# Two-block transformer on one core: the dense feed-forward products take the stream's high and low parts side by side

## The chip, the cores and the metric

One core of a Trainium2 chip runs the whole program in one launch. The metric is the device time of that core in microseconds; lower is better. The kernel before takes 2152.02 us, the median of three runs (2150.91 to 2152.64).

## What is computed

A sequence of 256 tokens of width 1024 goes through three layers. The first is a block with HGRN2 and block attention and a dense SwiGLU feed-forward of width 2816. The second layer has a mixer of four branches (pooling, short convolution, spatial gating, differential attention) and another dense feed-forward of 2816; the third has the same kind of mixer and a mixture of eight experts. Cut to what the change touches:

```
def swiglu(x, w_gate_up, w_down):
    g, u = jnp.split(x @ w_gate_up, 2, axis=-1)
    return (jax.nn.silu(g) * u) @ w_down
...
merged = (gates[:, :, 0] * (y_a @ w_branch_pool[layer])
          + gates[:, :, 1] * (y_b @ w_branch_conv[layer])
          + gates[:, :, 2] * (y_c @ w_branch_sgu[layer])
          + gates[:, :, 3] * (y_d @ w_branch_attn[layer]))
return merged @ w_out[layer]
```

All inputs are float32, and float32 precision is kept by splitting both operands of every large product into a rounded high part and a low remainder. A product is then three matmuls: weight-high with stream-high, weight-high with stream-low, weight-low with stream-high.

## The kernel before

**Weights.** Each weight element is used once. `load` brings 1 MB at a time into a raw buffer on SP's queue. `look_ahead` (line 417 is its subtraction, line 185 the helper that issues every ScalarE instruction) cuts a load into *pieces* of 1024 columns per partition: ScalarE copies a piece to `hi`, VectorE subtracts to get `lo`. Three pieces are kept ahead of TensorE, and `hi` and `lo` have four buffers each.

**Units.** The order of the work is written out by hand, with no scheduler: `unit` issues one piece's products, then the next piece's split, then whatever evacuations are pending (`flush`). A function put up with `defer` goes out one flush later. Each engine works its own list in that order and waits on semaphores for the others. Side work (attention heads, small mixers) is issued between units by generators.

**Dense feed-forward** (`ffn`, `residual`). The normalized stream `N.x` is held transposed, features on partitions, as four page pairs of high (`nh`) and low (`nl`), each 2 x 256 tokens. `chunk_t` makes 256 output columns: two pieces m = 0, 1 of 128 columns, for each of 8 contraction blocks k the three 256-column matmuls of `mm3t` (lines 502 to 504), with the weights as the stationary operand:

```
mm(out, hi[:, k, :], xh, start=r + k == 0, stop=False)
mm(out, hi[:, k, :], xl, start=False, stop=False)
mm(out, lo[:, k, :], xh, start=False, stop=r + k == kb - 1)
```

The two pieces lie in the two halves of one PSUM bank. There are 11 gate chunks and 11 up chunks in each of the two dense feed-forwards. The gate chunk is multiplied by the norm's factors (line 540) and goes through Silu; the up chunk is multiplied by them and by the gate (985), then split into `ah` and `al` (215). The first gate chunk, `chunk_late`, puts off its last two blocks, since the stream's last quarter comes late. `residual` then makes the down product over 22 blocks in four such chunks and adds each to the stream `self.x` (963), after which `norm_feed` prepares that quarter for the next norm. When `residual` ends an attention or mixer part instead (8 blocks), it begins with `chunk_late_pair` and feeds `ffn`.

**PSUM.** Eight banks: a pool of four that `gp` hands out (large products) and one of four that `sp` hands out (small products of heads, transposes, norms).

**Mixer's end** (`mixer`, `branch`, `gate_half`, line 565 to 567). The gates of the third and fourth branch's second half are still being made (`gate_half` holds two `gp` banks open over two units) while the four branch products run: `branch(0, 0)` and `branch(1, 0)` come between the two halves of gate 2. A branch takes two `gp` banks, 12 matmuls of 512 columns (24 for the fourth), and is evacuated one unit later by `gated` (line 916), which multiplies the gate with it:

```
gate_half(2, 0)
self.drain()
sigmoids(2)
branch(0, 0)
sigmoids(1)
branch(1, 0)
gate_half(2, 4, 1)
```

## Time and profile before

| | us |
|---|---|
| median of three runs | 2152.02 (2150.91 to 2152.64) |
| the profiled execution | 2152.17 |
| its span in the trace | 2150.4 |
| TensorE (PE) busy | 2134.0 (99%) |
| VectorE (DVE) busy | 1736.9 (81%) |
| ScalarE (ACT) busy | 1436.6 (67%) |
| granted TensorE clock, mean | 0.997 |

The span is what the trace covers; the profiled execution's own time has 1.8 us more around it. A row of the page's busy groups gives a line, engine, operation, output and inputs, the count, the busy time and the mean of one. Matmuls overlap, so a matmul's length in the trace is not its price: the distance from one start to the next is. In a matmul's row the moving operand stands first, then the stationary one.

### The profile page before, as it was taken

What the parts mean: (1) busy time and instruction counts of PE and PEld (TensorE: products, weight loads), DVE (VectorE), ACT (ScalarE), POOL (GpSimd) and SP (SyncE); (2) the same over time, 40 slices, a digit from 0 to 9 for tenths busy, and PEclk for the clock granted to TensorE, in tenths of its full rate; (3) what the DMA queues carried; (4) which work ended last, traced back from release to release, by engine and by line L of the source; (5) the groups of instructions that cost most, each with busy time, mean ns of one, the idle gap of its engine ahead of it and who ended that gap; (6) DMA issues with size and microseconds to landing.
All of it is one profiled execution on the core that took longest, in us unless ns stands there. A gap on an engine that the chain in (4) does not pass through costs nothing.

```text
span 2150.4 us, 32906 instructions
## 1 busy us (share of the span) xinstructions
PE 2134.0 (99%) x12243; PEld 1870.0 (87%) x12243; DVE 1736.9 (81%) x2424; ACT 1436.6 (67%) x2022; POOL 67.9 (3%) x90
## 2 busy tenths in 40 slices
PE   9999999999999999999999999999999999999998
PEld 9988889999987999999879788888888888888886
DVE  7877667655686766567867999999999999999997
ACT  6347645444556554445665888888887888888886
POOL 0000000003000000020000000000000000000200
PEclk9999999999999999999999999999999999999999
DMA  9444455546644555475475899999999999999995
GB/s 346 144 137 158 137 187 186 184 161 219 205 153 157 195 181 183 149 244 176 147 245 196 298 329 385 353 375 374 383 377 351 383 367 387 350 384 373 385 387 185
DMA packets 338280, 565.31 MB, mean 263 GB/s; under 512 B 14090, under 2 KB 117530, under 8 KB 338112
## 3 DMA queue, kind: packets, MB, share of 16 engines
q1 hardware_dynamic: 333616, 551.50, 73.7%
q0 software_dynamic: 4064, 11.05, 1.5%
q8 instruction: 98, 1.61, 0.3%
q10 hardware_dynamic: 432, 0.57, 0.1%
q14 instruction: 70, 0.57, 0.1%
HBM read 558.32 MB, written 4.75 MB: 262 GB/s over the span
## 4 chain that ended last, share of the span: by engine, by line
PE 97%; ACT 1%; DMA 1%; DVE 0%; issue 0%; SPq 0%; DVEq 0%; ACTq 0%
PE g L1755 9%; PE g L1757 9%; PE g L1756 9%; PE g L502 8%; PE g L503 8%; PE g L504 8%; PE g L565 7%; PE g L566 7%; PE g L567 7%; PE y L1778 5%; PE y L1779 5%; PE y L1780 5%; PE lev L1069 1%; PE at L1735 1%; PE xe L1674 1%; PE g L554 1%
## 5 line engine op out<-in xcount | busy, mean ns | idle before, releaser
L185 ACT ACTIVATE hi<-raw 128x1024 fp32r<-128x1024 f32 (+2 forms) x1223 | 1123.6, 934 | 586.1 <-PE g L503 196.8
L417 DVE TENSOR_TENSOR lo<-raw,hi 128x1024 fp32r<-128x1024 f32 (+2 forms) x1216 | 1273.5, 1074 | 237.5 <-ACT hi L185 202.4
L1755 PE MATMUL g<-hi,xe 128*128 128x512 f32 x896 | 353.8, 395 | 0.0
L1757 PE MATMUL g<-lo,xe 128*128 128x512 f32 x896 | 349.3, 390 | 0.0
L1756 PE MATMUL g<-hi,xe 128*128 128x512 f32 x896 | 349.0, 389 | 0.0
L502 PE MATMUL g<-nh,hi 128*128 128x256 f32 x1024 | 291.7, 285 | 0.0
L504 PE MATMUL g<-nh,lo 128*128 128x256 f32 x1024 | 289.8, 283 | 0.0
L503 PE MATMUL g<-nl,hi 128*128 128x256 f32 x1024 | 289.7, 283 | 0.0
L565 PE MATMUL g<-hi,nh 128*128 128x512 f32 x544 | 219.6, 404 | 0.2 <-DVE gt L916 0.2
L567 PE MATMUL g<-lo,nh 128*128 128x512 f32 x544 | 212.4, 390 | 0.0
L566 PE MATMUL g<-hi,nl 128*128 128x512 f32 x544 | 212.0, 390 | 0.0
L1757 PEld LDWEIGHTS g<-lo,xe 128*128 128x128 f32 x896 | 168.2, 188 | 35.9
L1756 PEld LDWEIGHTS g<-hi,xe 128*128 128x128 f32 x896 | 168.4, 188 | 33.4
L1755 PEld LDWEIGHTS g<-hi,xe 128*128 128x128 f32 x896 | 168.3, 188 | 33.4
L503 PEld LDWEIGHTS g<-nl,hi 128*128 128x128 f32 x1024 | 196.5, 192 | 0.2
L502 PEld LDWEIGHTS g<-nh,hi 128*128 128x128 f32 x1024 | 196.4, 192 | 0.2
L504 PEld LDWEIGHTS g<-nh,lo 128*128 128x128 f32 x1024 | 196.4, 192 | 0.0
L1778 PE MATMUL y<-hi,ah 128*128 128x512 f32 x448 | 175.8, 392 | 0.0
L1779 PE MATMUL y<-hi,al 128*128 128x512 f32 x448 | 174.5, 390 | 0.0
L1780 PE MATMUL y<-lo,ah 128*128 128x512 f32 x448 | 174.4, 389 | 0.0
L565 PEld LDWEIGHTS g<-hi,nh 128*128 128x128 f32 x544 | 102.4, 188 | 23.5 <-issue 3.2
L567 PEld LDWEIGHTS g<-lo,nh 128*128 128x128 f32 x544 | 102.1, 188 | 22.1
(421 smaller groups left out, 2797.2 us busy)
## 6 DMA issues: line engine op xcount, KB each, us to landing
raw<-in_moe_w_gate_up_dram SPq DMA_DIRECT2D x168, 1024.0 KB, 7.1
raw<-in_w_in_dram SPq DMA_DIRECT2D x90, 1024.0 KB, 5.1
raw<-in_moe_w_down_dram SPq DMA_DIRECT2D x88, 1024.0 KB, 5.9
raw<-in_moe_w_gate_up_dram SPq DMA_DIRECT2D x224, 256.0 KB, 7.2
raw<-in_moe_w_down_dram SPq DMA_DIRECT2D x96, 256.0 KB, 6.7
raw<-in_ffn_w_gate_up_dram SPq DMA_DIRECT2D x22, 1024.0 KB, 5.1
raw<-in_w_ffn_gate_dram SPq DMA_DIRECT2D x11, 1024.0 KB, 5.3
raw<-in_w_ffn_up_dram SPq DMA_DIRECT2D x11, 1024.0 KB, 5.4
```

The lines of the kernel that those rows point to most:

```text
L185: return self.nc.scalar.activation(out, in_, func, **kw)
L417: self.nc.vector.tensor_sub(l, x, h)
L502: mm(out, hi[:, k, :], xh, start=r + k == 0, stop=False)
L503: mm(out, hi[:, k, :], xl, start=False, stop=False)
L504: mm(out, lo[:, k, :], xh, start=False, stop=r + k == kb - 1)
L565: mm(ps[t], xh[:, s], hi[:, k, :], start=r + k == 0, stop=False)
L566: mm(ps[t], xl[:, s], hi[:, k, :], start=False, stop=False)
L567: mm(ps[t], xh[:, s], lo[:, k, :], start=False, stop=r + k == kb - 1)
L1755: mm(ps, xh, hi[:, k, :], start=first, stop=False)
L1756: mm(ps, xl, hi[:, k, :], start=False, stop=False)
L1757: mm(ps, xh, lo[:, k, :], start=False, stop=last)
L1778: mm(py, xh, hi[:, i, :], start=k == 0, stop=False)
```

## The change

The high and low part of the stream lie in one page, side by side (`gain` with `pairs`, `split_pair`), so that one 512-column matmul, `mm_hi`, makes weight-high with both parts; `mm_lo` then adds weight-low with stream-high, 256 columns, to the half that holds weight-high with stream-low. `chunk_pair` issues eight of the first and then eight of the second for a piece. Each piece has a bank of its own now, so a chunk holds two; `bank` takes one from each pool in turn. The two halves of a bank have to be added: in gate and up ScalarE copies one half out and VectorE adds the other (`halves`), in the down product (first three of four chunks) VectorE adds both halves to the stream. The fourth down chunk keeps `chunk_t`. Silu is put off by one more flush. In the mixers, `branch` takes its banks from the small products' pool.

```diff
--- before.py
+++ after.py
@@ -214,6 +214,18 @@
         self.copy(hi, x)
         self.defer(lambda: self.nc.vector.tensor_sub(lo, x, hi))
         return hi, lo
+
+    def split_pair(self, x):
+
+        pages = [self.pgv(2, T, dt=F32R, nm="a") for _ in range(2)]
+        for j, p in enumerate(pages):
+            self.copy(p[:, 0, :], x[:, j, :])
+
+        def rest():
+            for j, p in enumerate(pages):
+                self.nc.vector.tensor_sub(p[:, 1, :], x[:, j, :], p[:, 0, :])
+        self.defer(rest)
+        return pages
 
     def warm(self, n, x):
 
@@ -492,6 +504,9 @@
 
 
     def xb(self, x, k):
+        if isinstance(x[k // 2], list):
+            p = x[k // 2][k % 2]
+            return p[:, 0, :], p[:, 1, :]
         h, l = x[k // 2]
         return h[:, k % 2, :], l[:, k % 2, :]
 
@@ -512,22 +527,52 @@
                 self.unit(lambda hi, lo: self.mm3t(pv[:, m, :], hi, lo, x, r, min(8, kb - r), kb),
                           (lambda: evac(pv)) if last else None, width)
 
-    def chunk_late(self, x, evac, width=1):
-
-        ps = [self.gp()[:, :T] for _ in range(2)]
+    def mm_hi(self, out, hi, x, r, n):
+
+        for k in range(n):
+            p = x[(r + k) // 2][(r + k) % 2]
+            self.nc.tensor.matmul(out, hi[:, k, :], p.rearrange("p a t -> p (a t)"), start=r + k == 0, stop=False)
+
+    def mm_lo(self, out, lo, x, r, n, kb):
+
+        for k in range(n):
+            p = x[(r + k) // 2][(r + k) % 2]
+            self.nc.tensor.matmul(out[:, T:], lo[:, k, :], p[:, 0, :], start=False, stop=r + k == kb - 1)
+
+    def bank(self):
+        self.turns += 1
+        return self.sp() if self.turns // 2 % 2 else self.gp()
+
+    def chunk_pair(self, x, evac, kb=8):
+
+        ps = [self.bank() for _ in range(2)]
+
+        def products(hi, lo, m, r):
+            n = min(8, kb - r)
+            self.mm_hi(ps[m], hi, x, r, n)
+            self.mm_lo(ps[m], lo, x, r, n, kb)
+        for m in range(2):
+            for r in range(0, kb, 8):
+                last = m == 1 and r + 8 >= kb
+                self.unit(lambda hi, lo: products(hi, lo, m, r), (lambda: evac(ps)) if last else None)
+
+    def chunk_late(self, x, evac):
+
+        ps = [self.bank() for _ in range(2)]
         late = []
         for m in range(2):
-            run = self.stage(width)
-            hi, lo = self.ahead.pop(0)
-            self.mm3t(ps[m], hi, lo, x, 0, 6, 8)
-            late.append((hi, lo))
+            run = self.stage(1)
+            late.append(self.ahead.pop(0))
+            self.mm_hi(ps[m], late[m][0], x, 0, 6)
+            self.mm_lo(ps[m], late[m][1], x, 0, 6, 8)
             if m == 0:
                 self.look_ahead()
             self.flush()
             self.finish(run)
-        for k in range(6, 8):
-            for m, (hi, lo) in enumerate(late):
-                self.mm3t(ps[m], hi[:, k:, :], lo[:, k:, :], x, k, 1, 8)
+        for m, (hi, lo) in enumerate(late):
+            self.mm_hi(ps[m], hi[:, 6:, :], x, 6, 2)
+        for m, (hi, lo) in enumerate(late):
+            self.mm_lo(ps[m], lo[:, 6:, :], x, 6, 2, 8)
         self.look_ahead()
         self.pending.append(lambda: evac(ps))
 
@@ -609,8 +654,9 @@
                           (lambda i=i: evacs[i](ps[i])) if r else None, width)
 
 
-    def norm_begin(self, g):
+    def norm_begin(self, g, pairs=False):
         N = Norm()
+        N.pairs = pairs
         N.g, N.x = g, [None] * 4
         page = self.pg(nm="rs")
         N.rs, N.tmp = page[:, :T], page[:, T:]
@@ -629,12 +675,17 @@
     def gain(self, N, c):
 
         x = self.x[c]
-        hi, lo = N.x[c] = tuple(self.pgv(2, T, dt=F32R, nm="n" + s) for s in "hl")
+        if N.pairs:
+            N.x[c] = [self.pgv(2, T, dt=F32R, nm="n") for _ in range(2)]
+            hi, lo = ([p[:, i, :] for p in N.x[c]] for i in range(2))
+        else:
+            N.x[c] = tuple(self.pgv(2, T, dt=F32R, nm="n" + s) for s in "hl")
+            hi, lo = ([t[:, j, :] for j in range(2)] for t in N.x[c])
         gs = [N.g[:, 2 * c + j:2 * c + j + 1] for j in range(2)]
         for j in range(2):
-            self.copy(hi[:, j, :], x[:, j, :], scale=gs[j])
+            self.copy(hi[j], x[:, j, :], scale=gs[j])
         for j in range(2):
-            self.nc.vector.scalar_tensor_tensor(lo[:, j, :], x[:, j, :], gs[j], hi[:, j, :], op0=OP.mult, op1=OP.subtract)
+            self.nc.vector.scalar_tensor_tensor(lo[j], x[:, j, :], gs[j], hi[j], op0=OP.mult, op1=OP.subtract)
 
     def squares(self, N, c, e):
 
@@ -953,10 +1004,14 @@
 
     def residual(self, x, kb, g, between=None):
 
-        N = self.norm_begin(g)
+        N = self.norm_begin(g, kb == 8)
 
         def evac(c, ps):
-            if isinstance(ps, list):
+            if kb == KF and c < 3:
+                for h in (slice(T, 2 * T), slice(0, T)):
+                    for m in range(2):
+                        self.nc.vector.tensor_add(self.x[c][:, m, :], self.x[c][:, m, :], ps[m][:, h])
+            elif isinstance(ps, list):
                 for m in range(2):
                     self.nc.vector.tensor_add(self.x[c][:, m, :], self.x[c][:, m, :], ps[m])
             else:
@@ -965,7 +1020,7 @@
         if between:
             self.chunk_late_pair(x, [lambda ps, c=c: evac(c, ps) for c in range(2)], between)
         for c in range(2 if between else 0, 4):
-            self.chunk_t(x, lambda ps, c=c: evac(c, ps), kb)
+            (self.chunk_pair if kb == KF and c < 3 else self.chunk_t)(x, lambda ps, c=c: evac(c, ps), kb)
         self.flush(True)
         return N
 
@@ -974,19 +1029,33 @@
         act = []
         s = [None]
 
+        def halves(out, ps, then):
+
+            for m in range(2):
+                self.copy(out[:, m, :], ps[m][:, T:])
+
+            def rest():
+                for m in range(2):
+                    nc.vector.tensor_add(out[:, m, :], out[:, m, :], ps[m][:, :T])
+                nc.vector.tensor_tensor(out, out, N.bc, op=OP.mult)
+                then()
+            self.defer(rest)
+
         def evac_g(ps):
-            s[0] = self.pgv(2, T, nm="s")
-            self.scaled(s[0], ps, N)
-            self.act(s[0], s[0], AF.Silu)
+            g = s[0] = self.pgv(2, T, nm="s")
+            halves(g, ps, lambda: self.defer(lambda: self.act(g, g, AF.Silu)))
 
         def evac_u(ps):
-            u = self.pgv(2, T, nm="u")
-            self.scaled(u, ps, N)
-            nc.vector.tensor_mul(u, u, s[0])
-            act.append(self.split(u, "a"))
+            u, g = self.pgv(2, T, nm="u"), s[0]
+
+            def then():
+                nc.vector.tensor_mul(u, u, g)
+                act.append(self.split_pair(u))
+            halves(u, ps, then)
+        self.turns = 0
         for c in range(FF // 256):
-            (self.chunk_t if c else self.chunk_late)(N.x, lambda ps: N.then(lambda: evac_g(ps)))
-            self.chunk_t(N.x, lambda ps: N.then(lambda: evac_u(ps)))
+            (self.chunk_pair if c else self.chunk_late)(N.x, lambda ps: N.then(lambda: evac_g(ps)))
+            self.chunk_pair(N.x, lambda ps: N.then(lambda: evac_u(ps)))
         self.flush(True)
         return self.residual(act, KF, g)
 
@@ -1434,7 +1503,7 @@
 
         def branch(b, c, evac=True):
             x = (ya, yb, yc, yd)[b]
-            ps = [self.gp() for _ in range(2)]
+            ps = [self.sp() for _ in range(2)]
             n = 4 if b == 3 else 2
             for r in range(0, n, 2):
                 self.unit(lambda hi, lo: self.products_tok(ps, hi, lo, x, r, n),
```

How it moves instructions, at three places. **TensorE, one piece of a gate or up chunk.** Before, the rows of two of its eight blocks (`nh`, `nl` are the stream's parts, `hi`, `lo` the weights'):

```order
L502 MATMUL g_1296_8101<-nh_1224_7536,hi_1288_8036 128x256
L503 MATMUL g_1296_8101<-nl_1225_7537,hi_1288_8036 128x256
L504 MATMUL g_1296_8101<-nh_1224_7536,lo_1290_8064 128x256
L502 MATMUL g_1296_8101<-nh_1230_7587,hi_1288_8036 128x256
L503 MATMUL g_1296_8101<-nl_1231_7588,hi_1288_8036 128x256
L504 MATMUL g_1296_8101<-nh_1230_7587,lo_1290_8064 128x256
```

With the change, a piece (`n` is a page with both parts):

```order
L534 MATMUL s_1299_7530<-n_1248_7194,hi_1287_7463 128x512
L534 MATMUL s_1299_7530<-n_1249_7195,hi_1287_7463 128x512
L534 MATMUL s_1299_7530<-n_1254_7245,hi_1287_7463 128x512
L534 MATMUL s_1299_7530<-n_1255_7246,hi_1287_7463 128x512
L534 MATMUL s_1299_7530<-n_1263_7314,hi_1287_7463 128x512
L534 MATMUL s_1299_7530<-n_1264_7315,hi_1287_7463 128x512
L534 MATMUL s_1299_7530<-n_1269_7355,hi_1287_7463 128x512
L534 MATMUL s_1299_7530<-n_1270_7356,hi_1287_7463 128x512
L540 MATMUL s_1299_7530<-n_1248_7194,lo_1291_7491 128x256
L540 MATMUL s_1299_7530<-n_1249_7195,lo_1291_7491 128x256
```

Twenty-four products of 256 columns became eight of 512 and eight of 256; the next six rows are like the last two. The weight's low part is first needed after the eighth product instead of at the third.

**VectorE, the same chunks.** Before, around one up chunk (`s` is its gate):

```order
L417 TENSOR_TENSOR lo_1313_8254<-raw_1261_7836,hi_1311_8227 128x1024
L540 TENSOR_TENSOR u_1315_8258<-g_1305_8167,rs_1202_7406 128x512
L985 TENSOR_TENSOR u_1315_8258<-u_1315_8258,s_1308_8196 128x512
L417 TENSOR_TENSOR lo_1318_8288<-raw_1261_7836,hi_1314_8256 128x1024
L215 TENSOR_TENSOR al_1317_8262<-u_1315_8258,ah_1316_8261 128x512
```

With the change:

```order
L429 TENSOR_TENSOR lo_1312_7624<-raw_1246_7188,hi_1310_7602 128x1024
L1039 TENSOR_TENSOR u_1311_7604<-u_1311_7604,s_1299_7530 128x256
L1039 TENSOR_TENSOR u_1311_7604<-u_1311_7604,g_1300_7531 128x256
L1040 TENSOR_TENSOR u_1311_7604<-u_1311_7604,rs_1226_7064 128x512
L1052 TENSOR_TENSOR u_1311_7604<-u_1311_7604,s_1303_7552 128x512
L429 TENSOR_TENSOR lo_1319_7656<-raw_1258_7280,hi_1314_7628 128x1024
L226 TENSOR_TENSOR a_1315_7634<-u_1311_7604,a_1315_7634 128x256
L226 TENSOR_TENSOR a_1316_7635<-u_1311_7604,a_1316_7635 128x256
L429 TENSOR_TENSOR lo_1322_7681<-raw_1258_7280,hi_1320_7658 128x1024
```

The multiplication that read PSUM is now two additions of 256 that read it and a multiplication in SBUF; the subtraction that makes the low part is in two. They still stand between the splits of the weights.

**TensorE, the mixer's end in the second layer**, from `branch(0, 0)` (`yah`, `yal`) to `branch(1, 0)` (`ybh`, `ybl`). Before (each block's rows once, though there are two of them):

```order
L565 MATMUL g_1134_7053<-hi_1119_6986,yah_965_6260 128x512
L566 MATMUL g_1134_7053<-hi_1119_6986,yal_966_6261 128x512
L567 MATMUL g_1134_7053<-lo_1124_7014,yah_965_6260 128x512
L565 MATMUL g_1137_7072<-hi_1125_7016,ybh_977_6339 128x512
L566 MATMUL g_1137_7072<-hi_1125_7016,ybl_978_6340 128x512
L567 MATMUL g_1137_7072<-lo_1127_7035,ybh_977_6339 128x512
```

With the change:

```order
L610 MATMUL s_1158_6711<-hi_1143_6644,yah_989_5918 128x512
L611 MATMUL s_1158_6711<-hi_1143_6644,yal_990_5919 128x512
L612 MATMUL s_1158_6711<-lo_1148_6672,yah_989_5918 128x512
L610 MATMUL s_1161_6730<-hi_1149_6674,ybh_1001_5997 128x512
L611 MATMUL s_1161_6730<-hi_1149_6674,ybl_1002_5998 128x512
L612 MATMUL s_1161_6730<-lo_1151_6693,ybh_1001_5997 128x512
```

Before, `g_1137` has the bank that `g_1133` of `branch(0, 0)` had just filled, the other two of the pool being held by the open gate; with the change `s_1161` has a bank that no branch had used.

## Rows read from the trace of the kernel before

**Rows 1.** The page: busy time of the engines, and the chain that ended last, by engine.
```profile
PE 2134.0 (99%) x12243; PEld 1870.0 (87%) x12243; DVE 1736.9 (81%) x2424; ACT 1436.6 (67%) x2022; POOL 67.9 (3%) x90
...
PE 97%; ACT 1%; DMA 1%; DVE 0%; issue 0%; SPq 0%; DVEq 0%; ACTq 0%
```
**Rows 2.** Groups of TensorE instructions with shapes kept apart (busy us, mean ns of one): the first of the three products of `mm3t`, by input; the other two have the same counts.
```profile
L502 PE MATMUL g<-nh,hi 128*128 128x256 f32 x1024 | 291.7, 285 | 0.0
...
L502 PE MATMUL g<-ah,hi 128*128 128x256 f32 x352 | 99.6, 283 | 0.0
```
**Rows 3.** TensorE's timeline (start us, length us): the first and the last of the 48 matmuls of the first feed-forward's first chunk.
```profile
331.38 0.28 PE L502 MATMUL g<-nh,hi 128*128 128x256 f32 x1
...
337.02 0.28 PE L504 MATMUL g<-nh,lo 128*128 128x256 f32 x1
```
**Rows 4.** TensorE's timeline: two 512-column products of the mixer's end with nine others between them, then two of an expert with 25 others between them.
```profile
711.33 0.40 PE L566 MATMUL g<-hi,yal 128*128 128x512 f32 x1
...
713.64 0.39 PE L567 MATMUL g<-lo,yah 128*128 128x512 f32 x1
...
1500.02 0.39 PE L1757 MATMUL g<-lo,xe 128*128 128x512 f32 x1
...
1505.91 0.39 PE L1779 MATMUL y<-hi,al 128*128 128x512 f32 x1
```
**Rows 5.** Engines by stretch: gate and up of the first dense feed-forward, then its down product. Columns: stretch, its length, busy us (instructions) of PE, weight loads, DVE, ACT, POOL, granted TensorE clock, DMA share, GB/s.
```profile
331.40:459.20 127.80, 127.80 (x1064) 127.60 (x1063) 83.96 (x97) 63.08 (x72) 1.11 (x2) 1.00 0.56 178
459.20:522.50 63.30, 63.30 (x530) 63.30 (x529) 34.50 (x36) 28.31 (x34) 12.18 (x16) 1.00 0.61 198
```
**Rows 6.** Groups of VectorE instructions with shapes kept apart.
```profile
L417 DVE TENSOR_TENSOR lo<-raw,hi 128x1024 fp32r<-128x1024 f32 x864 | 1050.4, 1227 | 217.1 <-ACT hi L185 183.0 <-PE fl L1039 1.7
...
L540 DVE TENSOR_TENSOR u<-g,rs 128x512 f32<-128x512 f32 x22 | 15.2, 691 | 18.4 <-PE g L504 18.4
L215 DVE TENSOR_TENSOR al<-u,ah 128x512 fp32r<-128x512 f32 x22 | 15.1, 685 | 1.4 <-ACT ah L185 1.4
...
L961 DVE TENSOR_TENSOR x<-x,g 128x256 f32<-128x256 f32 x8 | 3.0, 415 | 0.0
...
L652 DVE TENSOR_TENSOR sq<-sq,sq 128x256 f32<-128x256 f32 x5 | 2.1, 425 | 0.5
```
**Rows 7.** Groups of ScalarE instructions with shapes kept apart.
```profile
L185 ACT ACTIVATE nh<-x,params 128x256 fp32r<-128x256 f32 x40 | 18.3, 498 | 13.6 <-DVE x L963 10.1 <-DMA params<-in_params_dram 2.0 <-DVE x L961 1.5
L185 ACT ACTIVATE ah<-u 128x512 fp32r<-128x512 f32 x22 | 13.9, 633 | 18.8 <-DVE u L985 18.8
...
L185 ACT ACTIVATE v<-g 128x256 f32<-128x256 f32 x16 | 4.8, 380 | 0.0
```
**Rows 8.** What TensorE waited for over the span: us in total, times, longest us.
```profile
PE g L565 <- ACT hi L185: 5.3, 2, 2.7
PE at L1735 <- DVE s L1747: 1.8, 3, 1.1
...
PE g L565 <- DVE gt L916: 0.2, 1, 0.2
```
**Rows 9.** TensorE's timeline around `branch(1, 0)` in the second and in the third layer: last product of `branch(0, 0)`, first of `branch(1, 0)`, first of the gate's second half.
```profile
678.80 0.39 PE L567 MATMUL g<-lo,yah 128*128 128x512 f32 x1
681.84 0.77 PE L565 MATMUL g<-hi,ybh 128*128 128x512 f32 x1 [2.65 <-ACT hi L185]
...
686.15 0.40 PE L565 MATMUL g<-hi,nh 128*128 128x512 f32 x1
...
1097.45 0.39 PE L567 MATMUL g<-lo,yah 128*128 128x512 f32 x1
1100.49 0.47 PE L565 MATMUL g<-hi,ybh 128*128 128x512 f32 x1 [2.65 <-ACT hi L185]
...
1104.90 0.40 PE L565 MATMUL g<-hi,nh 128*128 128x512 f32 x1
```
**Rows 10.** Engines by stretch, columns as in rows 5: `branch(1, 0)` in either layer, from its first product on.
```profile
681.80:685.20 3.40, 3.36 (x8) 2.74 (x9) 2.05 (x3) 0.02 (x1) 0.00 (x0) 0.52 0.81 273
1100.40:1104.40 4.00, 3.91 (x11) 3.18 (x12) 3.06 (x4) 0.07 (x1) 0.00 (x0) 0.63 0.92 286
```
**Rows 11.** ScalarE's timeline around the first of those waits.
```profile
676.69 2.19 ACT L185 ACTIVATE gt<-gt 128x512 f32<-128x512 f32 x4
678.79 1.04 ACT L185 ACTIVATE hi<-raw 128x1024 fp32r<-128x1024 f32 x1
```
**Rows 12.** VectorE's timeline: around the same wait, then at the mixer's tail (the evacuation of `branch(2, 1)`'s first bank).
```profile
679.87 1.23 DVE L417 TENSOR_TENSOR lo<-raw,hi 128x1024 fp32r<-128x1024 f32 x1 [2.63 <-ACT hi L185]
681.01 1.28 DVE L916 TENSOR_TENSOR gt<-gt,g 128x512 f32<-128x512 f32 x2
...
720.19 0.68 DVE L916 TENSOR_TENSOR gt<-gt,g 128x512 f32<-128x512 f32 x1
```
**Rows 13.** VectorE's timeline: the last quarter of the first feed-forward's input is made.
```profile
332.85 0.89 DVE L637 SCALAR_TENSOR_TENSOR nl<-x,params,nh 128x256 fp32r<-128x256 f32 x2 [0.58 <-ACT nh L185]
```
**Rows 14.** TensorE's timeline: the first products of `branch(3, 1)`, whose second bank is filled from the seventh on.
```profile
719.78 0.39 PE L565 MATMUL g<-hi,ydh 128*128 128x512 f32 x1
```
**Rows 15.** Engines by stretch, columns as in rows 5: before the experts, and the experts.
```profile
1130.00:1180.00 50.00, 49.99 (x351) 46.21 (x350) 39.11 (x74) 27.08 (x53) 0.00 (x0) 1.00 0.57 207
1181.00:2143.00 962.00, 959.40 (x4391) 794.44 (x4390) 899.45 (x1022) 791.97 (x975) 18.61 (x24) 1.00 0.99 358
```

## The prediction

> **What bounds the kernel now.** First the page's busy times and its chain: TensorE is busy 99% of the span and makes up 97% of the chain that ended last [rows 1]. So only what shortens TensorE's list of work, or a wait in it, can shorten the time; work added on VectorE or ScalarE costs nothing until TensorE waits for it. But busy is no price here: a 256-column product is 0.28 us long in the trace, while the 48 products of one chunk start between 331.38 and 337.02, which is 5.64 us over 47 steps, **0.120 us a step** [rows 3]. For 512 columns, 26 steps among the experts take 5.89 us, **0.2265 us a step**, and ten at the mixer's end 2.31 us, 0.231 [rows 4]. Twice 256 columns cost 0.240, so there is something paid per product: 512 columns cost 0.1065 more than 256, and 0.120 less 0.1065 leaves 0.0135 us for a product beside its columns.
>
> Next the stretches: in gate and up of a dense feed-forward TensorE runs without a gap for 127.80 us, at a granted clock of 1.00, with VectorE busy 83.96 us, ScalarE 63.08 and DMA at 0.56 of its share [rows 5]. Nothing but TensorE is near its end there.
>
> Last the waits: over the whole span the trace shows 5.3 us for products of line 565, in two waits, and little else [rows 8]. Their place is `branch(1, 0)` of either mixer [rows 9].
>
> **The change, term by term.**
>
> *Merged products.* In the two dense feed-forwards, gate and up are 2 x 22 chunks of 2 pieces and 8 blocks, 704 triples of products (among the 1024 on `nh`), and three of the four down chunks are 2 x 3 x 2 x 22 = 264 (of the 352 on `ah`) [rows 2]. For each of these 968 triples, three steps of 0.120 become one of 512 and one of 256 columns: 0.360 less 0.2265 less 0.120 is 0.0135 us. That gives 968 x 0.0135 = **13.1 us**. With the 512-column step of the mixer's end, 0.231, it would be 0.009 x 968 = 8.7 us. I take the experts' step, since it is from an unbroken run of products at full clock, as the feed-forward is [rows 4, 5].
>
> The Trainium skill (TensorE: Matmul & The Clock Gate, section on the back-to-back issue gap) gives a warm product N/2.4 ns plus a fixed 2.5 ns, and by that a removed product is worth a fifth of what I take: 968 x 2.5 ns, an estimated 2.4 us, and the total would be 2140.5 us. The trace disagrees with it by 0.0135 against 0.0025 us [rows 3, 4], so the measurement decides.
>
> *A wait in either mixer.* `branch(1, 0)` can only have the two `gp` banks that `branch(0, 0)` filled just before, as the open gate holds the other two. VectorE empties those at 681.01, and it is late because it works in order: ahead of it stands a weight's subtraction (679.87), which waits for ScalarE's copy (678.79), which stands behind four sigmoids (676.69) [rows 11, 12]. The table of waits names the ScalarE copy that ended at the same moment; nothing that `branch(1, 0)` reads was still missing. TensorE's next start is 681.84 instead of 678.80 + 0.2265, and after it the granted clock is 0.52 (0.63 in the third layer), that is, products at the lower of the two levels, 1.2 GHz, after TensorE had stood still [rows 9, 10]. Both together: with 13 steps of 0.2265 after 678.80 the gate's second half would start at 681.74, and it starts at 686.15, so 4.41 us; in the third layer 1100.39 against 1104.90, 4.51 us. With `sp` banks the first two branches have four banks of their own. The weights that come next are ready: TensorE needs the delayed piece only two units later, at about 684.5, and VectorE has it at 681.1. So I count all of it, and 0.2 us for the fourth gate, which waited for a branch's bank too [rows 8]: **9.1 us**.
>
> *What is added on VectorE and ScalarE.* For a gate and an up chunk, VectorE gets four additions of 256 that read PSUM (0.415 each) and two subtractions of 256 (0.425) for one of 512 (0.685): 1.83 us more, or 20.1 us for 11 pairs [rows 6]. It is then busy 104 us in the 127.80 - 352 x 0.0135 = 123.05 us that the stretch will last, 85%. ScalarE gets four copies of 256 out of PSUM (0.380) and two of 256 (0.498) for one of 512 (0.633): 1.88 us more, 20.7 in all, 83.8 of 123.05 us, 68% [rows 5, 7]. No bank is waited for: a chunk is evacuated within two units, and with eight banks at two per chunk a bank comes round after four chunks, eight units. In the down product VectorE has 34.50 of 63.30 us [rows 5] and gets one microsecond more per chunk. The cover of all this is TensorE's own work; if VectorE were the later one, its excess would come straight on top (rival 4). SP's and POOL's lists are the same, and DMA has 0.44 of its share free, so the faster use of weights is met.
>
> *The seams.* The first gate chunk now takes 12 x (0.2265 + 0.120) = 4.16 us before it needs the stream's last quarter, 0.16 less than before; it starts at 331.38 and needs that quarter at 335.5, which is made by 333.74 [rows 3, 13]. It now needs its low part at once too, but that is included in 333.74. At the end of up, the last chunk's way to the down product is two copies, two additions, two multiplications (0.69 each), two copies and two subtractions: 0.76 + 0.83 + 1.38 + 1.00 + 0.85 = 4.8 us; the down product comes to those blocks after 16 x 0.3465 + 4 x 0.2265 = 6.5 us. Both seams cost nothing, by 1.8 and 1.7 us. At the mixer's tail the four `sp` banks are shared with the transposes. The tightest place is `branch(3, 1)`: its second bank is that of `branch(2, 1)`'s first, which VectorE has read at 720.87, and TensorE comes to it at 719.78 + 6 x 0.2265 = 721.14 [rows 12, 14]. That holds by 0.27 us, and I count nothing.
>
> *The sum.* 13.1 + 9.1 = 22.2 us off the profiled execution's 2152.17 gives 2129.97. The median of the runs is 0.15 lower than that execution, so **2129.8 us**. What follows only moves forward in time: the experts start with the same buffers full, since DMA is at 0.57 of its share just before them [rows 15].
>
> **Rivals.**
>
> 1. *The bank wait moves to the mixer's tail.* The margin of 0.27 us goes if VectorE is one weight subtraction (1.23 us) later there. TensorE would then stand about 0.96 us in either mixer, and if the clock falls again, as after the other wait, 4.41 - 2.81 = 1.6 us more: 2 x 2.56 = 5.1, so 2134.9 us. For it: the margin. Against it: VectorE's list at that place is the same as before, so nothing makes it later. Chance 0.09.
>
> 2. *A product has no price beside its columns.* Then 512 columns cost two steps of 0.120, the merge gives nothing, and only the mixers' 9.1 us remain: 2142.9 us. The steps of 0.2265 and even 0.231 speak against it [rows 4]. The Trainium skill's 2.5 ns, above, lies near this case. Chance 0.03.
>
> 3. *The experts are bound by DMA.* In their 962 us DMA's share is 0.99 at 358 GB/s [rows 15]. If the weights' stream, not TensorE, set their end, and if it could not start earlier, the time would stay at 2152, no change. Against it: TensorE is busy 959.40 of the 962, its longest waits there are for the transposes' input, not for a weight [rows 8], and the stream starts at a place in the program that comes earlier as well. Chance 0.04.
>
> 4. *Slower: VectorE becomes the bound in gate and up.* It decides at 123.05/11 = 11.19 us of VectorE work for a pair of chunks; I have (83.96 + 20.1)/11 = 9.46. If the four additions took as long as a weight's subtraction (1.227), for waiting in the in-order list for ScalarE's copies, a pair would take 9.46 + 4 x 0.81 = 12.70, 1.51 us over, and 22 pairs would lose 33 us: 2163 us. Over 12.2 us a pair the kernel is slower than before. For it: VectorE goes from 66% to 85% in that stretch. Against it: three pieces are kept ahead, so a delay of the weights has two units, 5.5 us, before TensorE sees it. Chance 0.04.
>
> **How the numbers follow.** My forecast has the remaining 0.80. A measurement of this kernel can tell about 0.2%, 4.3 us, from no change. The forecast and rivals 1 and 2 are faster by more: 0.92; rival 3 is the same: 0.04; rival 4 slower: 0.04. The range: downward, the runs' spread of 0.9 us and the 1.8 us that experts' transposes waited for VectorE [rows 8], which may fall out otherwise: 2127. Upward, the 512-column step of 0.231 gives 2134.2 and rival 1 2134.9; either with the spread and some of the other is 2137. So 2127 to 2137.
>
> **What would show it.** Right: in gate and up 16 products a piece, 512-column ones starting 0.2265 apart, and the stretch about 4.8 us shorter in either feed-forward, its down product 1.8 us; no wait at `branch(1, 0)`, and a granted clock of 1.00 through it; VectorE near 104 us in the stretch. Wrong: a wait of TensorE for the additions of `halves` or for a split in gate and up; a wait at `branch(3, 1)` or at a transpose of the tail; waits of the experts for weights that were not there before; a step other than 0.2265.

## The result and the profile after

| | before | with the change |
|---|---|---|
| median of four runs, us | 2152.11 (2150.91 to 2152.64) | 2133.66 (2133.34 to 2134.1) |
| span of the profiled execution, us | 2150.4 | 2131.6 |
| granted TensorE clock, mean | 0.997 | 0.999 |

The ratio is 0.9915, interval 0.9898 to 0.9932: 18.45 us faster, where 22.2 were forecast. The four executions of the kernel before have a median of 2152.11; the 24 that ran beside the experiments below have medians of 2150.79 (of 9) and 2150.99 (of 15), against which the change is 17.1 to 17.3 us faster. Why they differ is told with `wait_filled`. The two traces are compared by stage, by the start of each stage's first product on TensorE: 331.38, 459.24, 522.60, 686.15, 1104.90 and the last at 2143.09 before, and 332.24, 456.32, 518.28, 677.42, 1086.50 and 2124.26 with the change.

| stage | forecast | measured |
|---|---|---|
| gate and up, each of two | -4.75 | -3.78 |
| first three down chunks, each of two | -1.78 | -1.40 |
| both feed-forwards | -13.1 | **-10.36** |
| mixer's end, second and third layer | -9.1 | **-9.36** (4.41 and 4.51 at `branch(1, 0)`; 0.32 and 0.12 at the third layer's fourth gate) |
| the program's first waits, up to 331 us | 0 | +0.86 |
| all, in the span | -22.2 | -18.83 |

From 1130 us to the end nothing but the shift is seen. First the engines by stretch, the two stretches of [rows 5] with the change, in the first and in the second feed-forward (columns as there):

```profile
332.24:456.32 124.08, 124.08 (x712) 109.09 (x711) 99.07 (x149) 75.16 (x124) 1.13 (x2) 1.00 0.56 183
456.32:518.28 61.96, 61.96 (x398) 56.39 (x397) 37.47 (x47) 29.32 (x37) 12.84 (x17) 1.00 0.60 204
740.45:864.53 124.08, 124.08 (x713) 109.09 (x711) 99.07 (x149) 75.16 (x124) 1.11 (x2) 1.00 0.56 182
864.53:926.49 61.96, 61.96 (x399) 56.40 (x397) 37.49 (x47) 29.32 (x37) 12.20 (x15) 1.00 0.60 202
```

TensorE is busy without a gap at a clock of 1.00, as before; no other engine has become the later one (VectorE 80%, ScalarE 61%, DMA 0.56). The stretch ends 124.08 us after its start and not, as forecast, 123.05. So the missing microsecond lies in the products themselves. TensorE's timeline over two pieces in gate and up (start us, length us; xN is a run of products alike):

```profile
400.46 2.00 PE L534 MATMUL g<-n,hi 128*128 128x512 f32 x8
402.30 1.11 PE L540 MATMUL g<-n,lo 128*128 128x256 f32 x8
403.25 2.00 PE L534 MATMUL s<-n,hi 128*128 128x512 f32 x8
405.09 1.12 PE L540 MATMUL s<-n,lo 128*128 128x256 f32 x8
406.04 0.40 PE L534 MATMUL s<-n,hi 128*128 128x512 f32 x1
```

"Long" are the products of 512 columns here, "short" those of 256. The eight long products take 402.30 - 400.46 = 1.84 us and not 8 x 0.2265 = 1.81; the eight short ones 0.95 and not 0.96. By the single starts, the steps after the eight long products' first, second and so on are 233, 236, 228, 233, 231, 227, 227 and 227 ns, the short ones' 113, 119 and then 120: 28 ns lost, 8 given back, 20 ns a piece.

The trace before had this already. There too 512-column products that follow shorter ones begin slowly, and the ten steps that gave the prediction its 0.231 [rows 4] are such a beginning, right behind four transposes of 128 columns:

```profile
710.66 0.60 PE L932 MATMUL mt<-consts,gt 128*128 128x128 f32 x4
711.01 0.48 PE L565 MATMUL g<-hi,yah 128*128 128x512 f32 x1
```

From 711.33 on the steps are 235, 234, 236, 224, 231, 235, 229, 232, 231 and 227 ns. From the thirteenth product of a run of 512-column products on, 4207 of 4255 steps before are under 230 ns. The slow beginning also follows a wait of TensorE: after `branch(1, 0)`'s wait in the third layer, for one, the second to fourth steps are 233, 236 and 236 ns.

At the mixers' end, the last product of `branch(0, 0)`, the first of `branch(1, 0)` and the first of the gate's second half, to hold against [rows 9]:

```profile
674.48 0.39 PE L612 MATMUL s<-lo,yah 128*128 128x512 f32 x1
674.70 0.39 PE L610 MATMUL s<-hi,ybh 128*128 128x512 f32 x1
...
677.42 0.39 PE L610 MATMUL g<-hi,nh 128*128 128x512 f32 x1
```

The engines over `branch(1, 0)` of the second and third layer, against [rows 10]:

```profile
674.70:677.40 2.70, 2.70 (x13) 2.25 (x12) 1.85 (x3) 2.70 (x4) 0.00 (x0) 1.00 0.00 0
1083.78:1086.50 2.72, 2.72 (x14) 2.25 (x13) 1.88 (x3) 2.72 (x5) 0.00 (x0) 1.00 0.00 0
```

From 674.48 on, thirteen steps of 0.2265 us follow one another, where there was a wait and then a clock of 0.52 and 0.63. The whole list of TensorE's waits, against [rows 8] (us in total, times, longest):

```profile
PE at L1804 <- DVE s L1816: 1.8, 3, 1.0
PE warm L746 <- DVE ones L787: 1.1, 1, 1.1
PE g L766 <- ACT hi L185: 1.0, 1, 1.0
PE po L1858 <- ACT yh L185: 0.7, 1, 0.7
PE g L766 <- ACT nh L185: 0.2, 1, 0.2
```

The waits of the branches are gone and none has come in their place. The third row is the program's first weights, at 10 us, and makes most of the 0.86 us by which everything starts later. It changes from kernel to kernel below without order, from 0.18 us earlier (`pairs_only`, which has the same feed-forwards) to 0.81 later (`four_four`), and is put down to the single execution, not to the change.

### The profile page after: what moved, and what is told of

Read it like the earlier page. It is cut to its first block, busy times and chain, and to the rows that moved or that the text cites. A ratio compares the mean times of both kernels' runs of the same rounds, so it can differ in the third digit from the quotient of the medians.

```text
span 2131.6 us, 31262 instructions
## 1 busy us (share of the span) xinstructions
PE 2119.8 (99%) x11275; PEld 1816.4 (85%) x11275; DVE 1772.5 (83%) x2550; ACT 1462.5 (69%) x2132; POOL 68.1 (3%) x90
## 3 DMA queue, kind: packets, MB, share of 16 engines
HBM read 558.32 MB, written 4.75 MB: 264 GB/s over the span
## 4 chain that ended last, share of the span: by engine, by line
PE 98%; DMA 1%; DVE 0%; SPq 0%; issue 0%; ACT 0%; DVEq 0%
PE g L1824 9%; PE g L1825 9%; PE g L1826 9%; PE g L610 7%; PE g L612 7%; PE g L611 6%; PE g L534 5%; PE s L534 5%; PE y L1847 5%; PE y L1848 5%; PE y L1849 5%; PE g L517 3%; PE g L519 3%; PE g L518 3%; PE s L540 3%; PE g L540 3%
## 5 line engine op out<-in xcount | busy, mean ns | idle before, releaser
L611 PEld LDWEIGHTS g<-hi,nl 128*128 128x128 f32 x544 | 102.4, 188 | 19.4
L1849 PEld LDWEIGHTS y<-lo,ah 128*128 128x128 f32 x448 | 84.1, 188 | 17.7
L1847 PEld LDWEIGHTS y<-hi,ah 128*128 128x128 f32 x448 | 84.2, 188 | 16.7
L1848 PEld LDWEIGHTS y<-hi,al 128*128 128x128 f32 x448 | 84.2, 188 | 16.5
L517 PE MATMUL g<-nh,hi 128*128 128x256 f32 x320 | 91.9, 287 | 0.0
L519 PE MATMUL g<-nh,lo 128*128 128x256 f32 x320 | 90.6, 283 | 0.0
```

Source lines behind the costliest of these rows:

```text
L611: mm(ps[t], xl[:, s], hi[:, k, :], start=False, stop=False)
L1847: mm(py, xh, hi[:, i, :], start=k == 0, stop=False)
L1848: mm(py, xl, hi[:, i, :], start=False, stop=False)
L1849: mm(py, xh, lo[:, i, :], start=False, stop=k == KE - 1)
```

## Experiments

Theory: the two gains are independent, the banks' 9.1 us at the mixers' end and some 10 to 13 us of the products; and what is missing of the products is lost where a run of short products turns to long ones. Rivals: the missing part is due to the new load of VectorE and ScalarE, to the alternating banks, or to 512-column products on these operands being slower throughout.

**One part at a time.** `mixer_banks_only` is the kernel before with one line of the change:

```diff
         def branch(b, c, evac=True):
             x = (ya, yb, yc, yd)[b]
-            ps = [self.gp() for _ in range(2)]
+            ps = [self.sp() for _ in range(2)]
```

> The kernel before with one edit: the mixers' branches take their banks from the small products' pool. Theory (the wait at branch(1, 0) was for a bank, and the clock fell because TensorE stood still): both waits and the slow products after them go, 4.4 + 4.5 us plus 0.3 us at the fourth gate, so 9.2 to 9.4 us less than before, 2142.8 us; granted clock 1.00 through branch(1, 0). Rival (the wait was for ScalarE's copy of a weight, as the table of waits names it): TensorE still stands 2.8 us at either place, no gain over 1 us.

Measured: 2142.86 us (2142.65 to 2143.37), ratio 0.9961 (0.9947 to 0.9974) to 2150.79 for the kernel before beside it: 7.9 us by the medians, where the trace gives 9.36. All of its TensorE's waits:

```profile
PE at L1735 <- DVE s L1747: 1.8, 3, 1.1
PE warm L695 <- DVE ones L736: 1.1, 1, 1.1
PE po L1789 <- ACT yh L185: 0.7, 1, 0.7
```

Both waits of line 565 are gone. By stage the mixers' ends become 4.41, 4.51, 0.32 and 0.12 us shorter, to the hundredth what the whole change shows there. That is shown: the wait was for the bank. The trace before has the lower clock after both waits, which not every execution has (see `wait_filled`); so the medians give less.

`pairs_only` is the change with that line put back:

> The changed kernel with one edit undone: the mixers' branches take their banks from the large products' pool again. Theory (the two parts add up): the dense feed-forwards' 10.4 us remain, of which 3.8 us in either gate-and-up stretch and 1.4 us in either down product, and the two waits of the mixers are back with 9 us: about 2142 us. Rival (the merged products were worth the 13.1 us that was predicted, and the other 2.7 us were lost to the mixers' use of banks or to the start): 2139 us, gate and up 4.75 us shorter.

Measured: 2142.64 us (2140.0 to 2144.44), ratio 0.996 (0.9947 to 0.9974); by stage -3.78 and -1.40 in either feed-forward, -10.36 in all, so the products' gain doesn't hang on the banks of the mixers. The waits are back, and this execution shows something more. TensorE's timeline at `branch(1, 0)` of the second layer, then of the third, and the engines over the branch in each:

```profile
673.43 0.39 PE L612 MATMUL g<-lo,yah 128*128 128x512 f32 x1
676.48 0.47 PE L610 MATMUL g<-hi,ybh 128*128 128x512 f32 x1 [2.65 <-ACT hi L185]
...
679.28 0.39 PE L610 MATMUL g<-hi,nh 128*128 128x512 f32 x1
...
1085.37 0.39 PE L612 MATMUL g<-lo,yah 128*128 128x512 f32 x1
1088.41 0.57 PE L610 MATMUL g<-hi,ybh 128*128 128x512 f32 x1 [2.65 <-ACT hi L185]
```
```profile
676.40:679.20 2.80, 2.72 (x12) 2.32 (x13) 2.71 (x4) 0.06 (x1) 0.00 (x0) 1.00 0.83 236
...
1088.40:1091.80 3.40, 3.39 (x9) 2.62 (x10) 2.24 (x3) 0.00 (x0) 0.00 (x0) 0.53 0.84 265
```

The same wait of 2.65 us, twice: after the first the clock stays at 1.00 and twelve steps end 2.80 us later; after the second it is 0.53. So the wait itself cost 2.8 us each time, and the slow products after it, 1.5 us of the 4.41 in the second layer before, came only after one of the two. The Trainium skill (TensorE: Matmul & The Clock Gate, section "What's actually happening") says that the gate's window runs free of the program, so that one kernel can meet it at another place each time; these two rows are in line with that, and show no more.

**What the missing part of the products is.** `alternate` has the same products in the order long, short, long, short:

```diff
-            self.mm_hi(ps[m], hi, x, r, n)
-            self.mm_lo(ps[m], lo, x, r, n, kb)
+            for k in range(n):
+                self.mm_hi(ps[m], hi[:, k:, :], x, r + k, 1)
+                self.mm_lo(ps[m], lo[:, k:, :], x, r + k, 1, kb)
```

> The changed kernel with the order within a piece changed: one 512-column product, one of 256, block by block, instead of eight and eight. Theory R (the first five long products after a run of short ones start 2 to 9 ns later than the others, because of the run): with no run, a pair takes 0.2265 + 0.120 = 0.3465 us, so 2.5 to 3 us less than the changed kernel, 2131 us. Rival S (every change from short to long costs some 20 ns whatever stands before it): about 840 changes more, 17 us more, 2150 us. Rival T (512-column products here take 0.231 us each by themselves): no difference.

Measured: 2131.05 us (2130.59 to 2132.73), ratio 0.9908 (0.9893 to 0.9923); gate and up -4.61, down -1.77, together -12.76 us. TensorE's timeline, five blocks, four pairs from the first to the last row:

```profile
400.26 0.39 PE L534 MATMUL g<-n,hi 128*128 128x512 f32 x1
400.49 0.28 PE L540 MATMUL g<-n,lo 128*128 128x256 f32 x1
...
401.65 0.39 PE L534 MATMUL g<-n,hi 128*128 128x512 f32 x1
```

Four pairs take 1.39 us, and the steps are 230 and 117 ns throughout: 346.7 a pair, which is 0.2265 + 0.120 as the prediction had it. VectorE, ScalarE and the banks do the same work as in the change, so neither they nor slow 512-column products are the cause; the order is. The long step alone is still 230 ns, but the short one's 117 gives that back, so only the pair's sum is a price.

`sixteen_sixteen` takes two pieces together, sixteen long products and then sixteen short ones (the first piece's low part is held back):

```diff
+            def first(hi, lo):
+                held.append(lo)
+                self.mm_hi(ps[m], hi, x, r, n)
+
+            def second(hi, lo):
+                self.mm_hi(ps[q], hi, x, s, c)
+                self.mm_lo(ps[m], held[0], x, r, n, kb)
+                self.mm_lo(ps[q], lo, x, s, c, kb)
```

> The changed kernel with two pieces taken together: sixteen 512-column products, then sixteen of 256; half as many changes from short to long, runs twice as long. Theories R and S: about 62 changes fewer at 20 ns, 1.2 us less than the changed kernel, 2132.4 us, the first five of sixteen long products later and the other eleven at 0.2265 apart. Rival T: no difference, all sixteen at 0.231 apart.

Measured: 2131.52 us (2130.96 to 2132.25), ratio 0.9908 (0.9893 to 0.9923); gate and up -4.17, down -1.58, together -11.50 us. Its timeline, from one sixteen to the next:

```profile
399.51 2.00 PE L534 MATMUL g<-n,hi 128*128 128x512 f32 x8
401.35 1.98 PE L534 MATMUL s<-n,hi 128*128 128x512 f32 x8
403.16 1.12 PE L540 MATMUL g<-n,lo 128*128 128x256 f32 x8
404.12 1.12 PE L540 MATMUL s<-n,lo 128*128 128x256 f32 x8
405.08 2.00 PE L534 MATMUL s<-n,hi 128*128 128x512 f32 x8
```

The first eight long products after short ones take 1.84 us, the next eight 1.81. With half as many changes from short to long, about half of the loss is gone: 1.14 us less by stage than with the change, where 1.2 were expected.

`four_four` goes the other way, four and four:

```diff
-            self.mm_hi(ps[m], hi, x, r, n)
-            self.mm_lo(ps[m], lo, x, r, n, kb)
+            for k in range(0, n, 4):
+                c = min(4, n - k)
+                self.mm_hi(ps[m], hi[:, k:, :], x, r + k, c)
+                self.mm_lo(ps[m], lo[:, k:, :], x, r + k, c, kb)
```

> The change, with a piece's products in four runs: four of 512, four of 256, four of 512, four of 256. With eight and eight, the first five 512-column steps after the short ones are longer (233, 236, 228, 233, 231 against 227 ns) and the short ones shorter at first, some 20 ns a piece; with one and one, nothing is lost (346.7 ns a pair); with sixteen and sixteen, half as much is lost a piece. What is open is whether the loss is paid for each change from short to long, or grows with the length of the short run. Theory A, a fixed loss for each change after more than a product or two: 40 ns a piece on some 124 pieces, 2.5 us more than eight and eight, 2136 us. Theory B, the loss grows in proportion to the short run before: four short ones lose 10 ns, twice a piece, so the same as eight and eight, 2133.7 us, with steps of about 230, 231, 228, 227 at the four positions. Theory C, only a long run of short products brings it on, and four are not enough: like one and one, 2131.1 us.

Measured: 2133.96 us (2133.46 to 2134.6), ratio 0.9918 (0.9905 to 0.9932); gate and up -3.50, down -1.31, together -9.62 us. Two fours take 1.40 us, against 1.39 for four pairs in turn:

```profile
400.55 1.09 PE L534 MATMUL g<-n,hi 128*128 128x512 f32 x4
401.48 0.64 PE L540 MATMUL g<-n,lo 128*128 128x256 f32 x4
401.95 1.09 PE L534 MATMUL g<-n,hi 128*128 128x512 f32 x4
```

Of the three theories C (no loss) falls, and A (2136) falls; B's time is met but not its steps: at the four positions they are mostly 230, 231, 236 and 228 ns. Set against one and one, over the 42 pieces of a gate and up whose order was changed (the first chunk's two pieces have the order of `chunk_late` in every run), a run of four loses (4.61 - 3.50) / 84 = 13.2 ns, a run of eight (4.61 - 3.78) / 42 = 19.8, a run of sixteen (4.61 - 4.17) / 21 = 21.0, near the 20 read from the steps. So the loss grows with the run and hardly beyond eight. Long and short runs were lengthened together, so which of the two it hangs on is not separated. What in TensorE makes it is open; the weight loads' records are 187 to 192 ns long in all orders.

**Is the slow clock from standing still?** `wait_filled` is the kernel before with spare products in the wait of the third layer alone:

```diff
             sigmoids(1)
+            if l:
+                self.warm(12, ya[0][0])
             branch(1, 0)
```

> The kernel before, with 12 spare 512-column products, whose result nothing reads, between branch(0, 0) and branch(1, 0) of the third layer alone. They need no bank that branch(1, 0) needs, and 12 x 0.2265 = 2.72 us fills the wait of some 2.8 us that branch(1, 0) has there. The theory that TensorE's low granted clock after the wait comes of its standing still: branch(1, 0) starts at the same moment, but its products run 0.2265 apart at a granted clock of 1.00, and the third layer's loss falls from 4.51 to about 2.85 us, so 1.6 us less for the program where the clock would else have fallen, 2149.2 us, and the runs scatter less; the second layer, untouched, keeps its 2.8 us wait and low clock. The rival, that the products after the wait are slow for what they read or where they write (weights just made, a bank just emptied): the clock and the slow steps stay as they were, and the time is unchanged or longer by the few tenths by which the spare products overrun the wait, 2150.8 to 2151.5 us. A further rival, that spare products take TensorE's time from the weights' preparation: none, since they use neither VectorE nor ScalarE.

Its timeline in the second layer, untouched, and in the third, and the engines over the branch in each:

```profile
679.12 0.39 PE L567 MATMUL g<-lo,yah 128*128 128x512 f32 x1
682.15 0.47 PE L565 MATMUL g<-hi,ybh 128*128 128x512 f32 x1 [2.65 <-ACT hi L185]
...
686.57 0.39 PE L565 MATMUL g<-hi,nh 128*128 128x512 f32 x1
...
1098.10 2.91 PE L222 MATMUL warm<-yah,ones_r 128*128 128x512 f32 x12
1100.91 0.47 PE L565 MATMUL g<-hi,ybh 128*128 128x512 f32 x1
...
1103.75 0.39 PE L565 MATMUL g<-hi,nh 128*128 128x512 f32 x1
```
```profile
682.10:685.50 3.40, 3.35 (x10) 2.66 (x11) 2.79 (x4) 0.04 (x1) 0.00 (x0) 0.64 0.87 271
...
1100.90:1103.70 2.80, 2.80 (x13) 2.33 (x13) 2.68 (x4) 0.00 (x1) 0.00 (x0) 1.00 0.76 233
```

In this execution the filled wait is followed by a clock of 1.00 and the third layer's branch takes 1.58 us less than before, as expected of standing still; the unfilled one is followed by 0.64. But `pairs_only` shows that an unfilled wait can be followed by 1.00 too, so one execution doesn't prove it, and the time doesn't: 2150.68 us (all but one run from 2148.71 to 2153.52), ratio 0.9998 (0.9988 to 1.0007), against 2149.2 expected. The interval reaches from 2.6 us faster to 1.5 slower, which holds the expected gain and no change alike. One run of 12178.66 us stands apart, which nothing here explains and which the ratio leaves out.

Each execution's mean clock says more. In the traces it is 0.997 where the clock fell after both waits (the kernel before), 0.998 where it fell after one (`pairs_only`, `wait_filled`) and 0.999 where there was no such fall (`mixer_banks_only`, the change). The 24 executions of the kernel before beside the experiments sort by it without overlap: 4 at 0.999 with a mean of 2148.9 us, 13 at 0.998 with 2150.8, 7 at 0.997 with 2152.9. That is some 2 us for each fall, and most of the scatter of 5 us. Read in the same way, the ten of `wait_filled` are 4, 5 and 1: 7 falls in 10 executions, where the kernel before had 27 in 24. That points to standing still and does not prove it: ten are few, and one of them has 0.997 with a single wait left. An execution of `alternate_all_down`, which has neither wait, shows 0.998 too, so the count is no more than a reading of the mean. Kernels with neither wait still scatter, over 0.7 us (`mixer_banks_only`) to 2.3 (`alternate_all_down`); that rest stays open.

**The best of it.** `alternate_all_down` is `alternate` with the fourth down chunk made like the other three (`kb == KF and c < 3` becomes `kb == KF` in both places):

> The change with long and short products alternating block by block, and the fourth down chunk made in the same way as the other three: 88 more triples of products at 0.360 - 0.3467 = 0.0133 us, 1.2 us less than with alternating alone, 2129.9 us, if nothing waits at the end of the down product. Theory of cover: the addition to the stream of the last chunk is now four additions of 256 in place of one of 512, about 1 us later, and what follows the feed-forward has products ready for that long. Rival: the end of the down product has no cover, since the next norm needs the last quarter; then the last quarter is 1 us late at both feed-forwards and the time is 2131.9 us, above alternating alone, with a new wait of TensorE after each down product.

Measured: 2129.8 us (2129.38 to 2131.68), ratio 0.9902 (0.9887 to 0.9918) to the 2150.99 of the kernel before beside it. The down product with its four chunks, and TensorE's timeline at its end and in the mixer after it:

```profile
455.10:516.12 61.02, 61.02 (x355) 53.80 (x354) 37.64 (x48) 29.34 (x37) 12.35 (x16) 1.00 0.62 205
```
```profile
516.00 0.28 PE L540 MATMUL g<-a,lo 128*128 128x256 f32 x1
516.12 0.39 PE L611 MATMUL g<-hi,nh 128*128 128x512 f32 x1
```

The down product is 2.35 us shorter than before instead of `alternate`'s 1.77, twice 0.58 = 1.16 us, and the next product follows after one step of 0.12: the cover held, no wait came. It beats the change by 3.9 us of median and has the lowest median of the kernels here, though the change and it were not run side by side.

## Why the prediction was right, and where it was off

*What bounds the kernel.* Right. TensorE's list and its waits were the time; VectorE went from 1736.9 to 1772.5 us of busy time and the kernel became faster.

*Merged products: mechanism right, size too large.* The step that failed is "I take the experts' step, since it is from an unbroken run of products at full clock, as the feed-forward is". Within a piece it is not unbroken: each run of eight short products is followed by five long steps above 0.2265. The experts' 26 steps begin at the fifteenth product of their run, past such a beginning, and the mixer's ten, 0.231, are one. The mean step of a triple was 0.360 - 3.78 / 352 = 0.3493 us in gate and up, so 0.0107 us saved and not 0.0135, and the term was 10.36 and not 13.1. The prediction's other end, 0.231, gives 8.7; it is what the 512-column products showed on the mean (0.2310 over the 704 of gate and up), but it leaves out what the short ones give back. With the order changed, 12.76 us came out, near the 12.9 of 968 triples at 0.360 - 0.3467. So the price of a product beside its columns, 0.0133 us, is shown for these products, each of which has a weight load of its own (11275 of either with the change); the two are not priced apart. The order gave 2.4 us of it away. By the 2.5 ns that the Trainium skill (TensorE: Matmul & The Clock Gate, section on the back-to-back issue gap) gives a warm product beside its columns, as the gap of an isolated one, an estimated 2.4 us would have come in all; the 12.76 measured decide against it here.

*The bank's wait.* Right in place and cause, and in size for the profiled execution: 4.41 and 4.51 as forecast, and 0.44 for what was put at 0.2. Where the clock doesn't fall, as once in `pairs_only`, a wait's price is 2.90. The forecast counts a fall after both waits, as the trace before has it; of the 24 later executions 7 read so. That the medians of the result are as far apart as 18.45 us is in part luck of the four executions before.

*VectorE and ScalarE.* Forecast 104 and 83.8 us in the stretch, measured 99.07 and 75.16. VectorE's added lengths were nearly right: its records in the stretch add up to 105.87 us against 86.62 before, 19.3 more where 20.1 were forecast. ScalarE's make 81.97 against 64.59, 17.4 more where 20.7 were forecast, mainly since its copies that split the up chunk's product take 0.410 us each and not the 0.498 of the rows that were taken for them. Beyond that, records of one engine overlap, and busy time counts an overlap once. In VectorE's timeline of one up chunk, the second addition starts 0.33 us after the first, which is 0.41 long, and two subtractions take 0.75 together:

```profile
402.00 0.41 DVE L1039 TENSOR_TENSOR u<-u,s 128x256 f32<-128x256 f32 x1
402.33 0.41 DVE L1039 TENSOR_TENSOR u<-u,g 128x256 f32<-128x256 f32 x1
...
405.32 0.75 DVE L226 TENSOR_TENSOR a<-u,a 128x256 fp32r<-128x256 f32 x2
```

That is the lesson that the prediction drew for TensorE, a record's length is not its price, and did not apply to VectorE. It cost nothing, since the error was on the safe side.

*The rivals.* Rival 1 (the wait moves to the mixer's tail) fell: `branch(3, 1)` comes to its second bank at 712.39, 0.27 us after VectorE has left it, with no wait. Rival 2 (no price beside the columns) fell, the triples being shorter by 0.0107 us with no change of clock. Rival 3 (DMA binds the experts) fell: the experts start earlier and end earlier by the same 18.83 us. Rival 4 (VectorE becomes the bound) fell, with VectorE at 80% and not one wait of TensorE for it in gate and up.

*The rest of the difference.* 2.7 us of products, 0.9 us of the program's first waits, less 0.3 us more than forecast at the mixers' end, are the 3.4 us by which the span fell short of 22.2; the medians' 3.75 has the other 0.4 us in the runs' scatter.

## What to carry to other kernels

A step taken from deep inside a run of like products is the price there and not at the run's beginning: where a change mixes long and short products, price the order too, and where the order is free, try them in turn. A wait on TensorE like the one here, of 2.65 us, is worth taking away for more than its length, since the products after it may run at the lower clock, and the runs scatter with that. And undo each half of a change alone: here the halves, 9.36 in `mixer_banks_only` and 10.36 in `pairs_only`, add up to the hundredth of a microsecond by stage, which shows that neither leans on the other. Their medians, 7.9 and 8.2 us, do not add up so well, since the clock falls in some executions and not in others: compare stages of traces that have had the same falls.

## What was not expected of the hardware

After a run of 256-column products the first five 512-column products start 233, 236, 228, 233 and 231 ns apart and then 227, the first two short ones after long ones 113 and 119 and then 120. In turns, the two kinds go at 230 and 117 with nothing lost in the sum. The loss was 0, 13.2, 19.8 and 21.0 ns for runs of one, four, eight and sixteen. And after one and the same wait of 2.65 us, in one execution, the granted clock was once 1.00 and once 0.53.
